# A decoder block on one core: fewer double seven-product units in FFN 1, one more in FFN 2, their products ordered by group, and three norms folded a step later

## The chip, the core and the metric

The kernel runs on one core of a Trainium2 chip. The metric is the device time of one execution in microseconds (us); lower is better. The core has a matrix engine (TensorE, PE in the profile, PEld for its weight loads), three elementwise engines (VectorE or DVE, ScalarE or ACT, GpSimd or POOL), and DMA queues, most of whose transfers are issued by SyncE (SP). Each engine works through its own instructions in their order and waits for the others by semaphores.

## The reference

One layer of a decoder block on 256 tokens of width 2048, in float32. What matters here are the two feed-forward parts at its ends, `h = h + 1/2 * SwiGLU(RMSNorm(h))`:

```python
def rms_norm(x, g):
    y = x * lax.rsqrt(jnp.mean(x * x, axis=-1, keepdims=True) + EPS)
    return y * g

def swiglu(x, w_gate, w_up, w_down):          # D_MODEL 2048, D_FF 5632
    return (jax.nn.silu(x @ w_gate) * (x @ w_up)) @ w_down
...
h = h + 0.5 * swiglu(rms_norm(h, ffn1_norm), ffn1_w_gate, ffn1_w_up, ffn1_w_down)
n = rms_norm(h, mix_norm)                     # retention and sliding-window attention, then w_out
h = h + memory_cross_attention(rms_norm(h, xa_norm), rms_norm(mem, mem_norm), ...)
h = h + 0.5 * swiglu(rms_norm(h, ffn2_norm), ffn2_w_gate, ffn2_w_up, ffn2_w_down)
```

## The kernel before

**Split operands.** Every operand of a matmul is split into a high half (a copy rounded to fp32r by ScalarE, L81) and a low half (what is left, by VectorE, L391). A product is three matmuls: high by high, high by low, low by high (`three`, L661 to 664). A weight arrives by DMA as a tile `wf` of 128x1024, and its split writes `wh` and `wl`.

**Steps.** All products stand in one long list of steps that `all_steps` (L336) makes. A plain step takes one weight tile, 2 token halves x 2 k-tiles x 3 = 12 matmuls of 128x512. `run_stream` (L404) walks the list. At each step it runs the tasks that are due, splits weights up to `LOOKAHEAD` = 3 steps ahead, issues loads up to 4 steps further ahead, then issues the step's matmuls. Tasks (`later`, L113) are pieces of work with a due time on a clock that counts 1 for a plain step and 0.5 for a chunk: copies, norms, transposes, sums. A scheduler then places the instructions on each engine.

**Units and twins.** The feed-forward parts work in units of 512 columns, 11 for gate and up and 4 for down. A `Twin` (L189) does gate and up of one unit (or two column blocks of down) together over four blocks of 512 rows of weights. A plain block costs 48 matmuls. One block, or two, is done in a seven-product way instead (Strassen's, in Winograd's form): it is seen as a 2 x 2 by 2 x 2 product (token halves, row halves, gate and up), which takes seven products, P1 to P7, each a chunk of 2 x 3 = 6 matmuls, 42 in all. For that VectorE forms differences of weights (L244, for P5, P6, P7 and P4), and seven tiles are split instead of four. P1, P3, P5 and P2 each load a tile; the others use differences. Sums of the inputs are made once per norm by `sums_of` (L309). After P1, P5, P6 and P7 of the last seven-product block, results are copied out of PSUM and added there (`keep`, `keep_other`, `middle`, `spread`, L272 to 286; adds on L265).

**Single and double units.** `sevens` (L740) is one block, or two when the unit's number is in `DOUBLE` (L39); the rest are plain. Chunks P1, P3, P5, P6, P7 of a unit are spread over the plain steps of the group ahead of it, P2 and P4 over its own (L363 to 372). `chunks` (L215) gives their order: kind by kind, and within a kind block by block. In FFN 1 `turned` is (2, 3), in FFN 2 (0, 1); units 4 and 8, which come right after a down part, are double in both.

**Norms.** `Norm.stat` sums squares on ScalarE and VectorE as blocks of `h` become ready. `Norm.finish` runs `delay` clock counts after the last of them: VectorE folds the sum (L593), TensorE adds over partitions with four tiny matmuls (L596), VectorE scales (L598), GpSimd takes the power -1/2 (L599). The matmuls of L596 stand in TensorE's order among the others, so TensorE waits there until the fold is done. The delays are 2 for `n1` (before FFN 1), 3 for `nmix` and 4 for `n2` (before FFN 2). The result is first used by the Silu of a gate (L710) or by a scaling copy.

Of the kernel before, what the change touches and what calls it, by code (L numbers as in the profile page):

```python
# [29 lines left out]
G_FFN1, G_MIX, G_XA, G_MEM, G_FFN2, G_GN = 0, 16, 32, 48, 64, 80  # L30
# [5 lines left out]
TURN = 6  # L36
SWA_EVERY = 4.5
LAND = 11
DOUBLE = (4, 8)  # L39
P1, P3, P5, P6, P7, P2, P4 = range(7)  # L40


# [1 line left out]
def decoder_block(ctx: ExitStack, tc: tile.TileContext, a: dict, out: bass.AP):  # L44
# [16 lines left out]
    def blk(dt=F32R):  # L61

        return work.tile([P, 4, 2, S], dt, tag="blk", name=nm("blk"), bufs=11)
# [4 lines left out]
    def t2k(dt=F32):  # L68
        return work.tile([P, 512], dt, tag="t2k", name=nm("t2k"), bufs=7)
# [10 lines left out]
    def copy(dst, src, **kw):  # L80
        return nc.scalar.activation(dst, src, AF.Copy, **kw)  # L81
# [31 lines left out]
    def later(delay, fn):  # L113
        tasks.append((clock[0] + delay, len(tasks), fn))
# [74 lines left out]
    class Twin:  # L189
# [23 lines left out]
            return self.plain[len(self.plain) - self.late :]  # L213

        def chunks(self, kinds):  # L215
            return [
                (self, c, None, kind, c == self.sevens[0], c == self.sevens[-1]) for kind in kinds for c in self.sevens
            ]

        def steps(self):  # L220
            return [
# [69 lines left out]
    def sums_into(s, v):  # L291

        for o, p, q, op in (
            (0, v(1, 0), v(1, 1), ALU.add), (1, s[:, 0], v(0, 0), ALU.subtract), (2, v(0, 0), v(1, 0), ALU.subtract),
            (3, v(0, 1), s[:, 1], ALU.subtract),
        ):
            dst = s[:, o]
            if len(q.shape) == 4:
                dst, p = (x.rearrange("p j (a b) -> p j a b", a=4) if len(x.shape) == 3 else x for x in (dst, p))
            elif len(p.shape) == 4:  # L300
                dst, q = (x.rearrange("p j (a b) -> p j a b", a=4) for x in (dst, q))
            nc.vector.tensor_tensor(dst, p, q, op)

    def split_sums(s):
        z = blk().rearrange("p k c s -> p (k c s)").rearrange("p (c i j s) -> p c i j s", c=2, i=4, j=2)
        halves(z[:, 0], z[:, 1], s)
        return z

    def sums_of(norm, b, dst, delay, src=None):  # L309

        y = [None]
        src = hT[b] if src is None else src

        def scale():
            y[0] = blk(F32).rearrange("p k c s -> p (k c s)")
            x = y[0][:, :1024].rearrange("p (j k s) -> p j k s", j=2, k=2)
            for k in range(4):
                g = norm.gcol + 4 * b + k
                copy(x[:, k % 2, k // 2, :], src[:, k, :], scale=gains[:, g : g + 1])

        def add():
            x = y[0][:, :1024].rearrange("p (j k s) -> p j k s", j=2, k=2)
            y.append(y[0][:, 1024:].rearrange("p (i j s) -> p i j s", i=4, j=2))
            sums_into(y[1], lambda t, k: x[:, :, k, t * P : (t + 1) * P])

        def part():
            dst[b] = split_sums(y[1])
        for i, fn in enumerate((scale, add, part)):
            later(delay + i, fn)

    def together(late=1):

        units[-2].then = units[-1]
        units[-2].late = units[-1].late = late
# [317 lines left out]
    def parts_of(x):  # L652
        return [x[:, :, c, :] for c in range(2)]

    def halves_of(out, x):
        for t in range(2):
            hi, lo = (y[:, :, t * P : (t + 1) * P].rearrange("p q (a j) -> p q a j", a=4) for y in x)
            halves(hi, lo, out[t])
        return x
# [35 lines left out]
    twins, input_sums = [], {}  # L695

    def twin(*args):

        twins.append(Twin(*args, ahead=bool(twins), spare=len(twins) % 2 == 0))

    def ffn(norm, w_gate, w_up, down, groups, turned):
        gated = {}
        made = {}
        acts = {}

        def gate_done(b, acc):
            assert norm.ready
            gated[b] = [t2k() for _ in range(2)]
            for t in range(2):
                nc.scalar.activation(gated[b][t], acc[t], AF.Silu, scale=norm.scale(t))  # L710

        def up_done(b, acc):
            s = gated.pop(b)
            for t in range(2):
                nc.vector.scalar_tensor_tensor(s[t], acc[t], norm.scale(t), s[t], ALU.mult, ALU.mult)
            turn(b, s)

        def both_done(b, f, acc):
            (gate_done, up_done)[f](b, acc)

        def turn(b, s):

            def made(out):
                acts[b] = blk()
                halves_of(out, parts_of(acts[b]))
                if b in starts:
                    y = blk(F32).rearrange("p k c s -> p (k c s)")[:, :1024].rearrange("p (i j s) -> p i j s", i=4, j=2)
                    sums_into(y, lambda t, k: out[t][:, 2 * k : 2 * k + 2])
                    asums[b] = split_sums(y)
            cross(s, made, TURN + (3 if b < 10 else 1))  # L730

        sums, asums = {}, {}
        twins.clear()
        input_sums[norm] = sums
        starts = [x[0] for x in groups]
        for g, fbs in enumerate(groups):
            for b in fbs:
                done = functools.partial(both_done, b)
                if b > 0:
                    sevens = turned[: 1 + (b in DOUBLE)]  # L740
                    plain = [x for x in range(4) if x not in sevens]
                    twin([w[2 * b : 2 * b + 2] for w in (w_gate, w_up)], norm.blocks, plain, sevens, sums, done)
                    if b == 1:
                        norm.bank = functools.partial(twins[0].bank, 0, 1)
                    continue
                for f, w in enumerate((w_gate, w_up)):
                    Unit(w, b, 512, norm.blocks, functools.partial(done, f), range(4), pair=True)
                if norm is not n1:
                    together(2)
            down(g, acts, fbs, asums)  # L750


    n1 = Norm(G_FFN1, "n1", 2)
    for b in range(4):
        if b > 0:
            later(4 * b - 1, lambda b=b: n1.block(b, [hT[b]]))
        later(4 * b + 2 * (b < 3), lambda b=b: n1.stat([hT[b]]))
    for at, b in ((8, 2), (40, 3)):
        later(at, lambda b=b: sums_of(n1, b, input_sums[n1], 0))

    def load_x(b, lo, hi):
        nc.sync.dma_start(hT[b][:, lo:hi, :], a["x"][b * P : (b + 1) * P, lo:hi, :])

    later(24, lambda: nc.sync.dma_start(sinks, a["sinks"]))

    nmix = Norm(G_MIX, "nmix", 3, spread=True)

    def near_mix(b):
        if b == 0:
# [6 lines left out]
    def ffn1_down(g, acts, fbs, sums):  # L776
        if g < 2:
            to_h(a["ffn1_w_down"], acts, 0.5, fbs, spare=3, seven=fbs[0], sums=sums)
        else:
            to_h(a["ffn1_w_down"], acts, 0.5, fbs, nmix, near_mix, seven=fbs[0], sums=sums)  # L780
            units[-2].rest = 4

    ffn(n1, a["ffn1_w_gate"], a["ffn1_w_up"], ffn1_down, (range(0, 4), range(4, 8), range(8, 11)), (2, 3))

# [400 lines left out]
    for i in range(4):  # L1187
        Unit(a["xa_wv"], i, 512, nmem.blocks, v_done(i), range(4))

    n2 = Norm(G_FFN2, "n2", 4)  # L1190
    to_h(a["xa_wo"], xo, 1.0, range(4), n2, lambda b: begin_ffn2(b), spare=2, seven=1, sums=osums, plain=2)
    units[-3].then, units[-3].lead = units[-2], 6

# [160 lines left out]
```

## Time and profile before

| | |
|---|---|
| Time, median of 3 runs | 2146.7 us (2138.54, 2146.7, 2147.3) |
| The profiled execution, its own time | 2140.22 us |
| its span | 2138.3 us |
| its mean granted TensorE clock | 0.997 |
| Instructions | 26847 |
| TensorE, busy | 2119.8 us, 99% of the span |
| VectorE, busy | 1698.5 us, 79% |
| ScalarE, busy | 1236.2 us, 58% |
| DMA | 482.61 MB, mean 226 GB/s |

In a row of the timeline the first two numbers are the start and the duration in us, then come engine, line and operation, tiles written and read without their numbers, shapes, and in brackets the idle time ahead of it on its engine and what ended it. In a row of waits: engine, tile and line that waited, what it waited for, the total, the number of times and the longest. The profile's line numbers are those of the kernel before.

### The profile page before, as it was taken

How to read it: one execution, taken by the hardware profiler on the slowest of the kernel's cores; microseconds unless marked ns; L12 is line 12 of the kernel's file. 1: busy time of each engine (PE TensorE's matmuls, PEld its weight loads, DVE VectorE, ACT ScalarE, POOL GpSimd, SP SyncE). 2: the span in 40 equal slices, each digit the busy share in tenths (PEclk: the TensorE clock that was granted, in tenths of full speed). 3: DMA queues.
4: the chain of work that ended last, by engine and by line, in shares of the span. 5: the costliest groups of instructions: out<-in, count | busy, mean ns of one | idle time of the engine just before them, and what ended most of it. 6: DMA issues, size and time to landing. Idle time of an engine off the chain costs nothing.

```text
span 2138.3 us, 26847 instructions
## 1 busy us (share of the span) xinstructions
PE 2119.8 (99%) x9564; PEld 1754.4 (82%) x9564; DVE 1698.5 (79%) x1997; ACT 1236.2 (58%) x1549; POOL 161.6 (8%) x273
## 2 busy tenths in 40 slices
PE   9999999999999999999999999999999999999998
PEld 7888788887888888878888888888888888888886
DVE  7887898778888788777887566578888888888875
ACT  6665565555666664546566454456666556555654
POOL 0000000000100210100101110011010000000000
PEclk9999999999999999999999999999999999999999
DMA  8677787777877876667878875586887677766773
GB/s 301 210 238 217 216 262 235 221 218 220 274 223 233 266 215 203 207 200 241 242 230 234 260 226 186 163 270 216 250 249 244 195 225 218 234 198 208 225 241 113
DMA packets 221286, 482.61 MB, mean 226 GB/s; under 512 B 18144, under 2 KB 18144, under 8 KB 221152
## 3 DMA queue, kind: packets, MB, share of 16 engines
q1 hardware_dynamic: 191312, 413.72, 61.6%
q0 software_dynamic: 12288, 33.57, 7.0%
q10 hardware_dynamic: 17552, 33.60, 4.3%
q8 instruction: 75, 1.23, 0.3%
q14 instruction: 59, 0.48, 0.1%
HBM read 445.17 MB, written 35.65 MB: 225 GB/s over the span
## 4 chain that ended last, share of the span: by engine, by line
PE 89%; DVE 5%; DMA 3%; issue 1%; ACT 1%; POOL 0%; DVEq 0%; ACTq 0%; POOLq 0%; SPq 0%
PE acc L664 55%; PE tmp L664 33%; DVE wl L391 2%; DMA wf<-in_ffn_w_up 1%; DMA wf<-in_ffn_w_gate 1%; DMA wf<-in_xa_wk 1%; ACT wh L81 1%; DVE blk L547 0%; DMA t4k<-box 0%; DMA wf<-in_ffn_w_down 0%; DVE t2k L585 0%; DVE h L679 0%; ACT blk L81 0%; DMA box<-t4k 0%; PE tmp L898 0%
## 5 line engine op out<-in xcount | busy, mean ns | idle before, releaser
L81 ACT ACTIVATE wh<-wf 128x1024 fp32r<-128x1024 f32 (+1 forms) x891 | 933.9, 1054 | 733.5 <-PE acc L664 416.6
L391 DVE TENSOR_TENSOR wl<-wf,wh 128x1024 fp32r<-128x1024 f32 (+1 forms) x886 | 1069.0, 1218 | 349.5 <-ACT wh L81 332.6
L664 PE MATMUL acc<-wh,blk 128*128 128x512 f32 (+1 forms) x3840 | 1211.8, 388 | 1.6 <-ACT wh L81 1.0
L664 PEld LDWEIGHTS acc<-wh,blk 128*128 128x128 f32 x3840 | 719.7, 188 | 151.4 <-ACT wh L81 2.0
L664 PE MATMUL acc<-wl,blk 128*128 128x512 f32 (+1 forms) x1920 | 744.5, 388 | 0.3 <-DVE wl L391 0.3
L664 PE MATMUL tmp<-wh,blk 128*128 128x512 f32 x2232 | 716.7, 390 | 0.0
L664 PEld LDWEIGHTS tmp<-wh,blk 128*128 128x128 f32 x2232 | 419.5, 188 | 87.5 <-ACT t2k L81 0.3
L664 PE MATMUL tmp<-wl,blk 128*128 128x512 f32 x1116 | 435.1, 390 | 2.5 <-DVE wl L391 2.5
L664 PEld LDWEIGHTS acc<-wl,blk 128*128 128x128 f32 x1920 | 361.8, 188 | 73.6 <-DVE wl L391 1.7
L647 POOL DMA_DIRECT2D t4k<-box x256 | 147.8, 584 | 1743.5 <-ACT wh L81 420.3
L664 PEld LDWEIGHTS tmp<-wl,blk 128*128 128x128 f32 x1116 | 209.8, 188 | 47.7 <-DVE wl L391 4.2
L244 DVE TENSOR_TENSOR wf<-wf,wf 128x1024 f32<-128x1024 f32 x152 | 185.9, 1223 | 31.3 <-DMA wf<-in_ffn_w_up 18.5
L81 ACT ACTIVATE t2k<-tmp 128x512 f32<-128x512 f32 x88 | 52.5, 597 | 33.6 <-PE tmp L664 21.1
L638 DVE STREAM_TRANSPOSE t4k<-t2k 128x512 f32<-128x512 f32 x96 | 64.5, 695 | 5.9 <-ACT t2k L81 5.5
L81 ACT ACTIVATE t2k<-acc 128x512 f32<-128x512 f32 x76 | 45.1, 596 | 29.7 <-PE acc L664 15.4
L86 DVE TENSOR_TENSOR blk<-t4k,blk 128x512 fp32r<-128x512 f32 (+2 forms) x72 | 44.3, 655 | 1.3 <-ACT blk L81 0.9
L81 ACT ACTIVATE blk<-t4k 128x512 fp32r<-128x512 f32 (+2 forms) x72 | 39.6, 595 | 3.3 <-DMA t4k<-box 2.6
L81 ACT ACTIVATE blk<-h,gains 128x256 fp32r<-128x256 f32 (+1 forms) x80 | 34.2, 496 | 11.6 <-DVE h L679 9.9
L265 DVE TENSOR_TENSOR tmp<-t2k,tmp 128x512 f32<-128x512 f32 x54 | 35.6, 690 | 0.0
L265 DVE TENSOR_TENSOR acc<-t2k,acc 128x512 f32<-128x512 f32 x48 | 31.7, 689 | 0.0
L547 DVE SCALAR_TENSOR_TENSOR blk<-h,gains,blk 128x256 fp32r<-128x256 f32 x64 | 26.8, 479 | 3.9 <-ACT blk L81 3.7
L679 DVE TENSOR_TENSOR h<-h,t4k 128x512 f32<-128x512 f32 x40 | 25.7, 684 | 2.7 <-DMA t4k<-box 2.7
(141 smaller groups left out, 607.7 us busy)
## 6 DMA issues: line engine op xcount, KB each, us to landing
wf<-in_ffn_w_gate SPq DMA_DIRECT2D x176, 512.0 KB, 5.1
wf<-in_ffn_w_up SPq DMA_DIRECT2D x176, 512.0 KB, 5.0
wf<-in_ffn_w_down SPq DMA_DIRECT2D x176, 512.0 KB, 4.6
box<-t4k ACTq DMA_DIRECT2D x64, 512.0 KB, 5.4
t4k<-box POOLq DMA_DIRECT2D x256, 128.0 KB, 7.1
wf<-in_w_in_rqk SPq DMA_DIRECT2D x32, 512.0 KB, 4.7
wf<-in_w_in_rvg SPq DMA_DIRECT2D x32, 512.0 KB, 4.7
wf<-in_w_out SPq DMA_DIRECT2D x32, 512.0 KB, 5.0
```

What stands on the lines that cost most here:

```text
L81: return nc.scalar.activation(dst, src, AF.Copy, **kw)
L86: nc.vector.tensor_tensor(lo, src, hi, ALU.subtract)
L244: nc.vector.tensor_tensor(dst, p, q, ALU.subtract)
L265: nc.vector.tensor_tensor(out, a, b, ALU.add)
L391: nc.vector.tensor_tensor(lo[:, cs], wf[:, cs], hi[:, cs], ALU.subtract)
L547: nc.vector.scalar_tensor_tensor(x[:, k, 1, :], v[:, k, :], g, x[:, k, 0, :], ALU.mult, ALU.subtract)
L638: nc.vector.transpose(z[:, t, :].rearrange("p (g q j) -> p q g j", g=4, q=4), squares_of(v))
L647: nc.gpsimd.dma_start(z[32 * g : 32 * g + 32].rearrange("p t (i n) -> p (t i) n", i=4), far[g])
L664: nc.tensor.matmul(o, x, y, start=first, stop=last, skip_group_check=shared)
L679: nc.vector.tensor_tensor(v, v, out[t], ALU.add)
```

## The change

Three things change. FFN 1 has one seven-product block in every unit (`turned` is (2,)), so its units 4 and 8 are no longer double, and the sums of its block 3 are no longer made. FFN 2 has a third double unit, 6. The chunks of a double unit come block by block (P1, P3, P5, P6 of the one, then of the other; P7 of both last), and so do P2 and P4. And the norms `n1`, `nmix` and `n2` have their `finish` one clock count later.

```diff
-DOUBLE = (4, 8)
+DOUBLE = (4, 6, 8)
...
         def chunks(self, kinds):
-            return [
-                (self, c, None, kind, c == self.sevens[0], c == self.sevens[-1]) for kind in kinds for c in self.sevens
-            ]
+            pairs = [(kind, c) for c in self.sevens for kind in kinds if kind != P7]
+            pairs += [(P7, c) for c in self.sevens if P7 in kinds]
+            return [(self, c, None, kind, c == self.sevens[0], c == self.sevens[-1]) for kind, c in pairs]
...
-                    sevens = turned[: 1 + (b in DOUBLE)]
+                    sevens = turned if b in DOUBLE else turned[:1]
...
-    n1 = Norm(G_FFN1, "n1", 2)
+    n1 = Norm(G_FFN1, "n1", 3)
...
-    for at, b in ((8, 2), (40, 3)):
-        later(at, lambda b=b: sums_of(n1, b, input_sums[n1], 0))
+    later(8, lambda: sums_of(n1, 2, input_sums[n1], 0))
...
-    nmix = Norm(G_MIX, "nmix", 3, spread=True)
+    nmix = Norm(G_MIX, "nmix", 4, spread=True)
...
-    ffn(n1, a["ffn1_w_gate"], a["ffn1_w_up"], ffn1_down, (range(0, 4), range(4, 8), range(8, 11)), (2, 3))
+    ffn(n1, a["ffn1_w_gate"], a["ffn1_w_up"], ffn1_down, (range(0, 4), range(4, 8), range(8, 11)), (2,))
...
-    n2 = Norm(G_FFN2, "n2", 4)
+    n2 = Norm(G_FFN2, "n2", 5)
```

Three places show how the instructions move. The first is TensorE at the statistic of `n1`, early in FFN 1. `acc` and `tmp` are PSUM tiles, `wh` and `wl` the halves of a weight, `blk` a block of the normed input. Before:

```order
L664 MATMUL acc_228<-wl_459,blk_423 128x512
L664 MATMUL acc_228<-wh_458,blk_423 128x512
L596 MATMUL tmp_469<-ones,t2k_216 128x1 x2
L664 MATMUL acc_228<-wh_458,blk_423 128x512
L664 MATMUL acc_228<-wl_459,blk_423 128x512
L664 MATMUL acc_228<-wh_458,blk_423 128x512
L664 MATMUL tmp_471<-wh_481,blk_402 128x512
```

Now the same stretch reads:

```order
L664 MATMUL acc_228<-wh_458,blk_423 128x512 x2
L664 MATMUL acc_228<-wl_459,blk_423 128x512
L664 MATMUL acc_228<-wh_458,blk_423 128x512
L664 MATMUL acc_160<-wh_497,blk_423 128x512
L664 MATMUL acc_160<-wl_498,blk_423 128x512
L664 MATMUL acc_160<-wh_497,blk_423 128x512 x2
L664 MATMUL acc_160<-wl_498,blk_423 128x512
L664 MATMUL acc_160<-wh_497,blk_423 128x512
L664 MATMUL acc_161<-wh_497,blk_423 128x512
L596 MATMUL tmp_469<-ones,t2k_216 128x1 x2
```

The statistic stands ten matmuls later, behind those with the low half `wl_498`, which came after it before.

The second is VectorE at the same place; L593 is the fold, L391 a low half, L244 a difference. Before:

```order
L244 TENSOR_TENSOR wf_432<-wf_432,wf_462 128x2x2x256
L391 TENSOR_TENSOR wl_498<-wf_464,wh_497 128x1024
L593 TENSOR_TENSOR t2k_216<-t2k_216 128x256
L391 TENSOR_TENSOR wl_517<-wf_432,wh_516 128x1024
L598 TENSOR_SCALAR ms_513<-tmp_469 128x2
```

Now:

```order
L244 TENSOR_TENSOR wf_432<-wf_432,wf_462 128x2x2x256
L391 TENSOR_TENSOR wl_498<-wf_464,wh_497 128x1024
L244 TENSOR_TENSOR wf_378<-wf_432,wf_378 128x2x2x256
L391 TENSOR_TENSOR wl_511<-wf_432,wh_510 128x1024
L593 TENSOR_TENSOR t2k_216<-t2k_216 128x256
```

A difference and a low half have moved ahead of the fold.

The third is VectorE in FFN 1's first down part, where the ahead chunks of unit 4 are made; `h` is the residual, to which a column block of down is added on L679. Before:

```order
L391 TENSOR_TENSOR wl_2060<-wf_1998,wh_2059 128x1024
L244 TENSOR_TENSOR wf_2131<-wf_2131,wf_1998 128x2x2x256
L391 TENSOR_TENSOR wl_2078<-wf_2016,wh_2077 128x1024
L391 TENSOR_TENSOR wl_2094<-wf_2033,wh_2093 128x1024
L244 TENSOR_TENSOR wf_2033<-wf_2033,wf_2097 128x2x2x256
L244 TENSOR_TENSOR wf_1950<-wf_2033,wf_1950 128x2x2x256
L391 TENSOR_TENSOR wl_2112<-wf_2051,wh_2111 128x1024
L679 TENSOR_TENSOR h_75<-h_75,t4k_1910 128x4x128 x2
```

Now the rows up to the same add:

```order
L391 TENSOR_TENSOR wl_2018<-wf_1938,wh_2017 128x1024
L391 TENSOR_TENSOR wl_2036<-wf_1969,wh_2035 128x1024
L391 TENSOR_TENSOR wl_2054<-wf_1986,wh_2053 128x1024
L391 TENSOR_TENSOR wl_2066<-wf_2004,wh_2065 128x1024
L391 TENSOR_TENSOR wl_2084<-wf_2021,wh_2083 128x1024
L679 TENSOR_TENSOR h_75<-h_75,t4k_1898 128x4x128 x2
```

The three differences ahead of the add are gone; the unit's one P5 difference stands eleven rows above the add, ahead of the low half `wl_1966`.

## The prediction

> **What bounds the kernel now.** I read the page first, then the table of waits of TensorE, then busy time by window, and last the timeline where TensorE waited. The page's first lines:
>
> ```profile
> span 2138.3 us, 26847 instructions
> PE 2119.8 (99%) x9564; PEld 1754.4 (82%) x9564; DVE 1698.5 (79%) x1997; ACT 1236.2 (58%) x1549; POOL 161.6 (8%) x273
> ```
>
> TensorE is busy in 99% of the span, so time can only come from fewer matmuls, from its 18.5 us of idleness, or from its clock. Its table of waits (total, times, longest):
>
> ```profile
> PE tmp L596 <- DVE t2k L593: 3.5, 3, 2.2
> PE tmp L664 <- DVE wl L391: 2.5, 4, 0.9
> ...
> PE acc L664 <- ACT t2k L81: 0.6, 1, 0.6
> ```
>
> The first row is the statistic of a norm, the second the low half of a weight, the third a copy out of PSUM. The windows show where the last two sit (length, then busy time of TensorE, its weight loads, VectorE, ScalarE and GpSimd with counts, granted clock, DMA share, GB/s):
>
> ```profile
> 100.00:150.00 50.00, 50.00 (x222) 41.42 (x221) 42.52 (x47) 31.85 (x39) 2.30 (x4) 1.00 0.76 228
> ...
> 1650.00:1700.00 50.00, 50.00 (x222) 41.40 (x221) 43.30 (x42) 28.44 (x29) 0.00 (x0) 1.00 0.60 190
> ...
> 1750.00:1800.00 50.00, 50.00 (x222) 41.42 (x221) 40.40 (x44) 29.55 (x33) 2.30 (x4) 1.00 0.79 227
> ...
> 250.00:255.00 5.00, 4.18 (x18) 3.30 (x18) 4.93 (x5) 2.37 (x3) 0.00 (x0) 1.00 0.48 140
> 255.00:260.00 5.00, 4.59 (x20) 3.62 (x20) 5.00 (x6) 2.29 (x3) 0.00 (x0) 1.00 0.35 107
> ...
> 275.00:280.00 5.00, 4.45 (x20) 3.36 (x20) 5.00 (x7) 3.32 (x5) 0.00 (x0) 1.00 0.73 229
> ...
> 500.00:505.00 5.00, 4.31 (x20) 3.22 (x18) 2.28 (x3) 3.00 (x4) 1.21 (x3) 1.00 1.04 261
> 505.00:510.00 5.00, 4.49 (x19) 3.37 (x19) 4.93 (x6) 2.36 (x3) 0.00 (x0) 1.00 0.37 111
> ```
>
> Undisturbed, TensorE issues 222 matmuls in 50 us, 0.2252 us each. In the five short windows the ahead products of FFN 1's double units 4 and 8 run, and TensorE idles for 0.82 + 0.41 + 0.55 + 0.69 + 0.51 = 2.98 us. Where those of FFN 2's unit 4 run (1650 to 1700) it does not idle.
>
> **Matmuls: +1.35 us.** A seven-product block issues 42 matmuls, a plain one 48. FFN 1 loses two such blocks, FFN 2 gains one: 6 more matmuls, 6 x 0.2252 = 1.35 us, all on the bound engine. There are 3 splits and 4 differences fewer.
>
> **FFN 1's double units: -2.98 us.** The timeline at unit 4:
>
> ```profile
> 248.40 1.23 DVE L244 TENSOR_TENSOR wf<-wf,wf 128x1024 f32<-128x1024 f32 x1 [2.08 <-DMA wf<-in_ffn_w_up]
> ...
> 250.82 0.50 PE L664 MATMUL tmp<-wl,blk 128*128 128x512 f32 x1 [0.87 <-DVE wl L391]
> ```
>
> The L244 is the second block's P5 difference. It held VectorE 2.08 us for a load, and the low half that TensorE wanted stood behind it. That instruction goes, and so do the differences that crowd VectorE at the adds to `h` after it (third place of the order). One P5 difference stays, earlier; it may wait for its own load, with a low half (`wl_1966`) behind it, but splits are made three steps ahead, 3 x 12 x 0.2252 = 8.1 us of TensorE's work. So I take all 2.98 us; the poor end is half of it.
>
> **The first norm: -3.1 us.** The timeline at its statistic, then the granted clock in quarters of a microsecond:
>
> ```profile
> 47.68 1.22 DVE L244 TENSOR_TENSOR wf<-wf,wf 128x1024 f32<-128x1024 f32 x1
> 47.87 0.40 PE L664 MATMUL acc<-wh,blk 128*128 128x512 f32 x1
> 48.81 1.22 DVE L391 TENSOR_TENSOR wl<-wf,wh 128x1024 fp32r<-128x1024 f32 x1
> ...
> 49.95 0.42 DVE L593 TENSOR_TENSOR t2k<-t2k 128x256 f32<-128x256 f32 x1
> ...
> 50.42 1.01 PE L596 MATMUL tmp<-ones,t2k 128*128 128x1 f32 x4 [2.16 <-DVE t2k L593]
> ...
> 51.29 0.77 PE L664 MATMUL acc<-wh,blk 128*128 128x512 f32 x1
> ...
> 51.71 1.62 POOL L599 TENSOR_TENSOR n<-ms,mhalf 128x2 f32<-128x2 f32 x1 [50.40 <-DVE ms L598]
> ...
> 57.34 0.62 PE L664 MATMUL acc<-wh,blk 128*128 128x512 f32 x2
> ...
> 57.84 0.69 ACT L710 ACTIVATE t2k<-acc,n 128x512 f32<-128x512 f32 x1 [0.78 <-PE acc L664]
> ```
>
> ```profile
> 50.25:50.50 0.25, 0.08 (x1) 0.08 (x1) 0.25 (x2) 0.00 (x0) 0.00 (x0) 0.83 0.40 156
> 50.50:50.75 0.25, 0.25 (x2) 0.25 (x2) 0.25 (x1) 0.00 (x0) 0.00 (x0) 0.50 0.74 287
> ...
> 57.00:57.25 0.25, 0.25 (x2) 0.25 (x1) 0.16 (x1) 0.06 (x1) 0.00 (x0) 0.51 0.97 303
> 57.25:57.50 0.25, 0.25 (x2) 0.21 (x2) 0.25 (x1) 0.00 (x0) 0.00 (x0) 1.00 1.04 311
> ```
>
> TensorE idles 2.16 us for the fold, which stands last in VectorE's backlog, and then the clock is halved from about 50.42 to 57.25, for 6.83 us. The two other statistics that TensorE waits for are those of `nmix` and `n2`:
>
> ```profile
> 744.99 0.61 PE L596 MATMUL tmp<-ones,t2k 128*128 128x1 f32 x4 [0.58 <-DVE t2k L593]
> ...
> 1467.01 0.58 PE L596 MATMUL tmp<-ones,t2k 128*128 128x1 f32 x4 [0.72 <-DVE t2k L593]
> 1467.45 0.48 PE L664 MATMUL tmp<-wh,blk 128*128 128x512 f32 x1
> ```
>
> The low clock costs: 14 matmuls between 51.29 and 57.34 took 6.05 us instead of 14 x 0.2252 = 3.15, and the statistic's own took 0.87 until the next matmul instead of 0.44 (at 1467.01): 2.90 + 0.43 = 3.3 us.
>
> The new order (first and second place) puts ten matmuls ahead of the statistic, 2.25 us, and a difference and a split ahead of the fold. It does not remove the wait. Of the ten, three run to about 48.77 and a fourth needs only a high half; the fifth needs the low half that VectorE ends at 48.81 + 1.22 = 50.03: a first wait of about 1.1 us. Six matmuls then end near 51.45. VectorE, busy throughout, begins an instruction every 1.14 us (48.81 to 49.95), so the fold begins at 49.95 + 2 x 1.14 = 52.23 and ends at 52.65: a second wait of about 1.25 us. Together 2.35 us, 0.19 more than before, but in two pieces with 1.35 us of matmuls between.
>
> What the clock makes of that no row shows. If it is judged by stretches of half the low time, 3.41 us, a stretch could before hold all 2.16 us of the gap; now the fullest holds 3.41 - 1.35 = 2.06, and when a border falls between the pieces, only some 1.2. So the bounds are 0.19 - 3.3 = -3.1 us (the clock holds) and +0.2 (it falls as before). I take -3.1, since most places of the border leave a stretch clearly less idle than the one that led to the half clock. The power on GpSimd ended at 51.71 + 1.62 = 53.33 and will end some 2.3 us later; its first reader, the gate's Silu, began at 57.84, so that hides.
>
> [...]
>
> **The other norms: -0.58 us.** For `nmix` the statistic stands 11 matmuls later (2.48 us) and the fold one split later (1.14 us): the wait of 0.58 us goes. For `n2` it is 20 matmuls (4.50 us) against 2 splits and 2 differences (4.56 us): the 0.72 us stay, 0. What else moves with a fold (the scaling, GpSimd's power, for `nmix` the spreading) moves by the same step.
>
> **FFN 2's third double unit and the order by groups: 0.** Unit 6's extra ahead products fall into 1750 to 1800: 5 splits and 3 differences, 8 x 1.14 = 9.1 us of VectorE beside 30 matmuls, 6.8 us. (40.40 + 9.1) / 56.8 = 87%, as in 1650 to 1700 (43.30 of 50), where nothing waits. That row is the nearest; the far end is unit 4 of FFN 1, 0.82 + 0.41 + 0.55 = 1.78 us. By groups, the six loads of a double unit are no longer in a row, and at most four differences follow each other instead of six: nothing waits in FFN 2's double units now, so there is nothing to gain; the far end is one wait like the 0.87 us above; 0 taken. The sums of FFN 1's fourth block, left out, ran beside a busy TensorE: 0.
>
> **Sum:** 1.35 - 2.98 - 3.1 - 0.58 + 0 = -5.3 us. The profiled execution took 2140.22 us, 6.5 below the median of the runs shown; I move the median: 2146.7 - 5.3 = **2141.4 us**.
>
> **Rivals.** *The clock still falls.* Either two waits of 2.35 us together are enough, or a wait of 2 us is not what halves the clock at all, and its cause stays. For it: 2.06 is hardly less than 2.16. Against: the border between stretches, and that the clock fell in the very quarter in which the wait ended. 2141.4 + 3.3 = 2144.7; chance 0.27. [...]
>
> *The waits only move.* VectorE loses 7 x 1.14 = 8 us of 1698.5; if its backlog is the cause, TensorE meets it elsewhere, and only the six matmuls count: 2146.7 + 1.35 = 2148.0; 0.13.
>
> *Slower: FFN 2's double units halve the clock.* If VectorE there falls back by 2.16 us in one place, that costs 2.16 + 3.3 = 5.5 us. One place takes the gain (+0.2); from the second on it decides: -5.3 + 11.0 = +5.7, 2152.4. For it: three double units and 87%. Against: no wait there now. 0.05.
>
> **How the numbers follow.** Forecast 0.5, the rivals 0.27, 0.13 and 0.05, 0.05 for the rest. The runs shown lie between 2138.54 and 2147.3, so a median can fall by that much by itself. Low end: the lowest run with the sum, and the waits left at `n1` and `n2` partly gone too: 2138.54 - 5.3 - 2.2 = 2131. High end: the second rival with 1.78 for the third double unit: 2150. A measurement can tell about 0.5%, 10.7 us, from no change. No case but the last rival doubled comes there by itself; the forecast does if the median falls at the lower end of the runs: faster 0.17, same 0.79, slower 0.04.
>
> **What would show it.** Right: no wait of TensorE near 250 and 505; two waits of about 1.1 and 1.25 us near 50, then clock 1.00; none near 745; no waits of TensorE between 1700 and 1825. Wrong: clock 0.50 after 52; waits on `wl` in FFN 2; a wait of 2 us or more at one place.

## The result, and the profile after

| | before | after |
|---|---|---|
| Median (lowest to highest) | 2143.38 us (2138.54 to 2147.3), 5 runs | 2160.5 us (2154.87 to 2165.0), 5 runs |
| The profiled execution, its span | 2140.22, 2138.3 us | 2154.87, 2153.1 us |

The change makes the kernel slower by a ratio of 1.0082 (95% interval 1.0055 to 1.0109), 17 us; 5 us faster was forecast. The profiled execution is the shortest of the five and 14.65 us above that of before. The first lines of the changed kernel's page, then its group of differences below that of the kernel before (count, busy time, mean ns of one, and the idle time of VectorE just ahead of them with what ended it):

```profile
span 2153.1 us, 26835 instructions
PE 2122.5 (99%) x9570; PEld 1754.5 (81%) x9570; DVE 1687.5 (78%) x1985; ACT 1229.7 (57%) x1541; POOL 159.6 (7%) x273
```

```profile
L244 DVE TENSOR_TENSOR wf<-wf,wf 128x1024 f32<-128x1024 f32 x152 | 185.9, 1223 | 31.3 <-DMA wf<-in_ffn_w_up 18.5 <-DMA wf<-in_xa_wk 6.6 <-DMA wf<-in_ffn_w_gate 2.2
L244 DVE TENSOR_TENSOR wf<-wf,wf 128x1024 f32<-128x1024 f32 x148 | 180.8, 1222 | 42.7 <-DMA wf<-in_ffn_w_up 31.8 <-DMA wf<-in_xa_wk 5.0 <-DMA wf<-in_ffn_w_gate 1.8
```

The counts are as costed: six matmuls more. VectorE has less to do than before and yet makes TensorE wait longer: it stands idle for 42.7 us ahead of its differences instead of 31.3, and 31.8 of them instead of 18.5 are for loads of the up weights. TensorE's table of waits:

```profile
PE tmp L664 <- DVE wl L391: 9.7, 3, 4.2
PE acc L664 <- DVE wl L391: 5.2, 5, 1.8
PE tmp L596 <- DVE t2k L593: 1.8, 2, 0.9
PE acc L664 <- ACT t2k L81: 1.6, 3, 1.1
```

The low halves went up from 2.5 us, the statistics of the norms went down from 3.5. To see where, I cut both spans at the same events, the product of up and gate (L715) of a unit. The windows from FFN 1's unit 3 to 4, 4 to 8, and FFN 2's unit 4 to 7; first before:

```profile
189.49:318.29 128.80, 126.97 (x558) 104.13 (x557) 110.01 (x111) 76.05 (x85) 11.51 (x20) 1.00 0.78 237
318.29:572.05 253.76, 252.56 (x1112) 208.10 (x1111) 211.90 (x215) 149.78 (x167) 18.43 (x32) 1.00 0.77 233
...
1735.94:1861.50 125.56, 125.56 (x555) 103.97 (x554) 101.95 (x106) 73.66 (x82) 6.91 (x12) 1.00 0.75 225
```

and after:

```profile
186.53:321.51 134.98, 129.44 (x559) 106.30 (x558) 102.50 (x104) 72.54 (x81) 11.50 (x20) 0.97 0.75 226
321.51:582.26 260.75, 255.13 (x1117) 210.49 (x1116) 204.54 (x209) 146.68 (x163) 18.41 (x32) 0.99 0.75 226
...
1748.21:1875.69 127.48, 124.79 (x549) 102.67 (x548) 109.52 (x113) 76.51 (x85) 6.91 (x12) 1.00 0.72 222
```

Up to unit 3 the changed kernel is 189.49 - 186.53 = 2.96 us ahead. Then the first down part with unit 4 takes 6.18 us more, the stretch to unit 8 with the second down part 6.99, FFN 2's third double unit 1.92; what lies between adds the rest. In the first of these TensorE idles 134.98 - 129.44 = 5.54 us (1.83 before), in the second 5.62 (1.20 before). Here is the first down part, on SyncE, VectorE and TensorE:

```profile
228.80 0.37 SPq L381 DMA_DIRECT2D wf<-in_ffn_w_up  x1
...
229.75 0.71 DVE L638 STREAM_TRANSPOSE t4k<-t2k 128x512 f32<-128x512 f32 x1 [0.36 <-ACT t2k L81]
...
233.91 0.84 PE L664 MATMUL tmp<-wh,blk 128*128 128x512 f32 x3
...
236.59 1.23 DVE L244 TENSOR_TENSOR wf<-wf,wf 128x1024 f32<-128x1024 f32 x1 [6.12 <-DMA wf<-in_ffn_w_up]
...
237.73 1.22 DVE L391 TENSOR_TENSOR wl<-wf,wh 128x1024 fp32r<-128x1024 f32 x1
...
239.00 0.80 PE L664 MATMUL tmp<-wl,blk 128*128 128x512 f32 x1 [4.25 <-DVE wl L391]
```

The difference at 236.59 is unit 4's P5. Its load was issued at 228.80. VectorE arrived at 230.47, 1.7 us later, and stood 6.12 us. The low half behind it needed nothing from that load (its high half, by the order of the splits, was ready at 230.67); it came at 238.95, and TensorE waited 4.25 us for it. The clock then:

```profile
235.00:237.50 2.50, 0.00 (x0) 0.00 (x0) 0.91 (x1) 1.34 (x2) 0.60 (x2) 0.95 0.59 225
237.50:240.00 2.50, 1.00 (x2) 0.83 (x3) 2.50 (x4) 0.00 (x0) 2.50 (x5) 0.50 0.65 167
240.00:242.50 2.50, 2.50 (x7) 1.98 (x6) 2.50 (x4) 0.00 (x0) 1.50 (x3) 0.50 0.89 257
242.50:245.00 2.50, 2.50 (x9) 1.96 (x8) 1.05 (x1) 0.90 (x1) 0.00 (x0) 0.69 1.07 235
```

It is at 0.50 from 237.23 to 244.06, while TensorE waits and for some 5 us more. The same pair stands in the second down part: VectorE waits 5.72 us for unit 8's P5 at 497.64, TensorE 3.85 us at 500.06. Units 5 and 9 add waits of 1.29 and 1.77 us at 285.12 and 545.86.

Before, the two P5 differences of unit 4 ran as follows (the second was shown with the prediction):

```profile
234.91 0.37 SPq L381 DMA_DIRECT2D wf<-in_ffn_w_up  x1
...
239.64 0.37 SPq L381 DMA_DIRECT2D wf<-in_ffn_w_up  x1
```

```profile
241.69 1.23 DVE L244 TENSOR_TENSOR wf<-wf,wf 128x1024 f32<-128x1024 f32 x1 [2.08 <-DMA wf<-in_ffn_w_up]
```

VectorE came to them at 239.61 and 246.32, 4.7 and 6.7 us after their loads had been issued, and waited 2.08 us for each. In all three cases the data came 6.8 to 8.8 us after the issue; the changed kernel's page has a median of 4.9 us for the loads of the up weights.

The norms, on TensorE of the changed kernel: the statistic of `n1`, and those of `nmix` and `n2`:

```profile
50.22 0.50 PE L664 MATMUL acc<-wl,blk 128*128 128x512 f32 x1 [0.99 <-DVE wl L391]
...
52.82 0.61 PE L596 MATMUL tmp<-ones,t2k 128*128 128x1 f32 x4 [0.93 <-DVE t2k L593]
...
758.62 0.59 PE L596 MATMUL tmp<-ones,t2k 128*128 128x1 f32 x4
...
1481.75 0.50 PE L664 MATMUL acc<-wl,blk 128*128 128x512 f32 x1 [0.96 <-DVE wl L391]
...
1483.31 0.58 PE L596 MATMUL tmp<-ones,t2k 128*128 128x1 f32 x4 [0.83 <-DVE t2k L593]
```

At `n1` two waits of about 1 us stand in place of 2.16, and the clock stays at 1.00. At `nmix` nothing waits. At `n2` a wait on a low half has joined the one on the fold. FFN 2's third double unit has two waits that no double unit had before:

```profile
1771.24 0.50 PE L664 MATMUL tmp<-wl,blk 128*128 128x512 f32 x1 [1.57 <-DVE wl L391]
...
1795.77 0.50 PE L664 MATMUL acc<-wh,blk 128*128 128x512 f32 x1 [1.11 <-ACT t2k L81]
```

### The profile page after: what moved, and what is told of

Its sections match the earlier page's. It is cut to its first block, busy times and chain, and to the rows that moved or that the text cites. A ratio compares the mean times of both kernels' runs of the same rounds, so it can differ in the third digit from the quotient of the medians.

```text
span 2153.1 us, 26835 instructions
## 1 busy us (share of the span) xinstructions
PE 2122.5 (99%) x9570; PEld 1754.5 (81%) x9570; DVE 1687.5 (78%) x1985; ACT 1229.7 (57%) x1541; POOL 159.6 (7%) x273
## 4 chain that ended last, share of the span: by engine, by line
PE 89%; DVE 4%; DMA 4%; issue 2%; ACT 1%; POOL 0%; SPq 0%; DVEq 0%; ACTq 0%; POOLq 0%
PE acc L664 55%; PE tmp L664 33%; DVE wl L391 2%; DMA wf<-in_ffn_w_up 2%; DMA wf<-in_ffn_w_gate 1%; ACT wh L81 1%; DMA t4k<-box 0%; DVE wf L244 0%; DMA box<-t4k 0%; DMA h<-in_x 0%; PE tmp L897 0%; DVE blk L547 0%; PE tmp L878 0%; DVE h L679 0%; PE tmp L971 0%
## 5 line engine op out<-in xcount | busy, mean ns | idle before, releaser
L391 DVE TENSOR_TENSOR wl<-wf,wh 128x1024 fp32r<-128x1024 f32 (+1 forms) x883 | 1064.9, 1218 | 357.3 <-ACT wh L81 344.9
L244 DVE TENSOR_TENSOR wf<-wf,wf 128x1024 f32<-128x1024 f32 x148 | 180.8, 1222 | 42.7 <-DMA wf<-in_ffn_w_up 31.8
L679 DVE TENSOR_TENSOR h<-h,t4k 128x512 f32<-128x512 f32 x40 | 25.7, 683 | 3.5 <-DMA t4k<-box 3.5
```

What stands on the lines that cost most here:

```text
L244: nc.vector.tensor_tensor(dst, p, q, ALU.subtract)
L391: nc.vector.tensor_tensor(lo[:, cs], wf[:, cs], hi[:, cs], ALU.subtract)
L679: nc.vector.tensor_tensor(v, v, out[t], ALU.add)
```

## The experiments

The theory after these traces: the scheduler puts a difference far ahead of the split that needs it; where the difference reads a tile that its own chunk has just loaded, VectorE stands still for the load, and everything behind it is late. I call that hoisting. The rivals: the order by groups, the third double unit or the delayed norms make the loss; or each wait is local and can be mended by itself.

**FFN 1's single units alone**, on the kernel before:

```diff
-    for at, b in ((8, 2), (40, 3)):
-        later(at, lambda b=b: sums_of(n1, b, input_sums[n1], 0))
+    later(8, lambda: sums_of(n1, 2, input_sums[n1], 0))
...
-                    sevens = turned[: 1 + (b in DOUBLE)]
+                    sevens = turned if b in DOUBLE else turned[:1]
...
-    ffn(n1, ..., (range(0, 4), range(4, 8), range(8, 11)), (2, 3))
+    ffn(n1, ..., (range(0, 4), range(4, 8), range(8, 11)), (2,))
```

> The kernel before with one part of the change alone: FFN 1 with single units only. Theory (in FFN 1 the P5 difference of units 4 and 8 now stands far ahead in VectorE's order, waits about 6 us there for its load, TensorE waits about 4 us behind it, and the clock halves): this part alone costs 2 x 7 = 14 us against before, waits of TensorE of 3.5 to 4.5 us near 235 and 495, VectorE idle 5 to 6 us on a load ahead of each. Rival (the loss is made in FFN 2 by the third double unit, or by the folds): -1.6 us or no change, and no wait of TensorE over 1 us in FFN 1 but at the first norm.

Measured: 2159.85 us against 2140.76 for the kernel before on the same chip, ratio 1.0087 (1.0075 to 1.0099). TensorE's waits:

```profile
PE tmp L664 <- DVE wl L391: 7.1, 2, 3.6
PE acc L664 <- DVE wl L391: 5.3, 2, 2.7
```

They stand at 237.63 (3.61), 284.00 (2.59), 500.19 (3.47) and 546.78 (2.68 us), each behind a P5 difference that VectorE waited for (5.49, 4.46, 5.34 and 4.55 us): those of units 4, 5, 8 and 9. This part alone makes a loss as large as the whole change's: 0.0087 x 2140.76 = 19 us, of which the twelve matmuls more (9576) are an estimated 12 x 0.2252 = 2.7. The theory's 14 us did not count units 5 and 9.

**The changed kernel with FFN 1's double units back:**

```diff
-                    sevens = turned if b in DOUBLE else turned[:1]
+                    sevens = turned if b in (DOUBLE if norm is not n1 else (4, 8)) else turned[:1]
```

with the sums of block 3 and (2, 3) as before.

> The changed kernel with FFN 1's units 4 and 8 double again, all else as changed (order by groups, third double unit in FFN 2, folds one step later). Theory: the two long waits in FFN 1 go, 14 us less than the changed kernel, so within 5 us of before. Rival (FFN 2 or the folds): stays about 17 us above before.

Measured: 2146.49 us, ratio 1.0018 (1.0006 to 1.003). Most of the 17 us is gone. 0.0018 x 2140.76 = 3.9 us are left, and the largest row of waits is a new one, on ScalarE's copies out of PSUM:

```profile
PE acc L664 <- ACT t2k L81: 6.0, 5, 1.8
```

**Two differences held.** In the changed kernel the P5 differences of FFN 1's units 4 and 8 may not go ahead of the VectorE instruction written just before them:

```diff
+            last, n = look(), seen[0]
             nc.vector.tensor_tensor(dst, p, q, ALU.subtract)
+            if kind == P5 and self.hold:
+                for ins in nc.cur_bb.bb.instructions[n:]:
+                    if ins.engine in anchored and ins.engine in last:
+                        order(last[ins.engine], ins)
...
+                    twins[-1].hold = norm is n1 and b in (4, 8)
```

`look` gives the last instruction of each engine so far, `order` keeps two in their order.

> The changed kernel with one more rule: the P5 differences of FFN 1's units 4 and 8 may not be placed ahead of the VectorE instruction that the program issues before them, which moves each about 11 rows later, behind ten low halves. Nothing else changes. Theory (the place of the difference is the cause): VectorE waits less than 1 us for each load, the waits of TensorE of 4.25 and 3.85 us and the low clocks behind them go, 10 to 14 us less than the changed kernel. Rival (the load itself is late, wherever the difference stands): the wait moves to the place of the P5 product or its split, TensorE still waits 2 us or more near 240 and 500, and the time stays within 4 us of the changed kernel.

Measured: 2151.68 us, ratio 1.005 (1.0037 to 1.0064). No wait is left near 237 and 500, but unit 5's P5 difference now waits longer, first on VectorE, then on TensorE:

```profile
277.13 1.23 DVE L245 TENSOR_TENSOR wf<-wf,wf 128x1024 f32<-128x1024 f32 x1 [5.09 <-DMA wf<-in_ffn_w_up]
```

```profile
279.55 0.79 PE L669 MATMUL acc<-wl,blk 128*128 128x512 f32 x1 [3.22 <-DVE wl L396]
```

Unit 9 does the same (2.56 us at 538.12). FFN 2's third double unit, which the edit leaves alone, shows a wait of 3.11 us on a copy at 1791.68 (1.11 in the changed kernel), after a difference that VectorE waited 3.26 us for. About half came back, and in FFN 1 the waits moved to the next hoisted differences. That each wait can be mended by itself is out.

**All differences held**, in the changed kernel: the same edit without its condition.

> The changed kernel with that rule for every difference: each now stands 1 to 6 rows ahead of its own split instead of 3 to 21. Theory: besides the two waits of FFN 1, VectorE's other waits for loads (5.0 us at the first unit of FFN 2, 4.0 us at the third double unit) shrink, and with them most of the waits of TensorE in FFN 2: at or below before, 14 to 20 us less than the changed kernel. Rival (a difference so near to its split stands in the way of it): new waits of TensorE at the products P5 to P7, time between before and the changed kernel or above.

Measured: 2132.3 us, ratio 0.996 (0.9948 to 0.9972): below both kernels, and (1.0082 - 0.996) x 2140.76 = 26 us below the change as it was. The group of differences (L244 is L245 here) and the two windows that hold the 4 us waits in the changed kernel:

```profile
L245 DVE TENSOR_TENSOR wf<-wf,wf 128x1024 f32<-128x1024 f32 x148 | 180.2, 1218 | 0.0
```

```profile
200.00:250.00 50.00, 50.00 (x222) 41.44 (x221) 39.62 (x40) 29.12 (x34) 4.62 (x8) 1.00 0.81 242
450.00:500.00 50.00, 50.00 (x222) 41.43 (x221) 38.88 (x39) 29.03 (x34) 6.93 (x12) 1.00 0.78 250
```

VectorE waits for no load ahead of a difference any more (42.7 us before the edit), and TensorE does its full 222 matmuls in 50 us. In VectorE's order, unit 4's P5 stood eleven rows ahead of the add to `h`; held, it stands two rows behind it, and begins at 247.77, 17.1 us after its load was issued (230.68).

**The three norms alone**, on the kernel before (the three delays, nothing else):

```diff
-    n1 = Norm(G_FFN1, "n1", 2)
+    n1 = Norm(G_FFN1, "n1", 3)
...
-    nmix = Norm(G_MIX, "nmix", 3, spread=True)
+    nmix = Norm(G_MIX, "nmix", 4, spread=True)
...
-    n2 = Norm(G_FFN2, "n2", 4)
+    n2 = Norm(G_FFN2, "n2", 5)
```

> The kernel before with the three norms' folds one step later and nothing else. Theory (the delays do what the prediction says of them): two waits of about 1 us near 50 us and no half clock after them, no wait at the statistic of nmix near 745, the one at n2 as before; -0.24 - 3.3 - 0.58 = -4.1 us against the kernel before, a ratio of about 0.998. Rival (the loss of the whole change has a share here, since each fold shifts differences and splits behind it): a wait of 2 us or more somewhere in the three stages and a ratio of 1.000 to 1.002.

Measured: 2138.86 us against 2140.49, ratio 0.9986 (0.9976 to 0.9996), so 0.9 to 5.1 us. Near 50 the waits are 0.92 and 0.95 us with the clock at 1.00, none is left at `nmix`, and the one at `n2` is 0.83. The theory stands. The profile also has waits outside the three norms, the longest 1.98 us at 1039.37 in the cross-attention with 3.41 us of half clock behind it: VectorE had stood 8.27 us there at a difference for a load of `in_xa_wk`. In the kernel before the same place has 6.59 us on VectorE and 0.31 on TensorE.

**The third double unit alone**, on the kernel before, in its order by kind:

```diff
-                    sevens = turned[: 1 + (b in DOUBLE)]
+                    sevens = turned[: 1 + (b in DOUBLE + (6,) * (norm is not n1))]
```

> The kernel before with FFN 2's unit 6 made double, in the old order by kind, and nothing else. Theory (the waits of 1.57 and 1.11 us that the changed kernel shows at its third double unit come from the order by groups and from a difference put far ahead): six matmuls fewer, no wait over 0.5 us between 1700 and 1830, -1.35 us, a ratio of 0.999. Rival (the double unit itself is too much for VectorE there): waits of 1.5 to 3 us there and +0.5 to +2 us, a ratio of 1.000 to 1.001.

Measured: 2142.35 us, ratio 1.0001 (0.9989 to 1.0013). Between 1700 and 1830 there is one wait, of 0.35 us at 1772.84. So the unit by itself makes no waits of the kind seen in the changed kernel; its 1.35 us are below what the runs can tell. Far from unit 6, the profile has a wait of 3.54 us at the statistic of `nmix` (746.53), which is no difference's: the fold was late because an add to `h` ahead of it had waited 3.22 us for a DMA (`t4k<-box`), where the kernel before waited 0.25.

**The order by groups alone**, on the kernel before:

```diff
-            return [
-                (self, c, None, kind, c == self.sevens[0], c == self.sevens[-1]) for kind in kinds for c in self.sevens
-            ]
+            pairs = [(kind, c) for c in self.sevens for kind in kinds if kind != P7]
+            pairs += [(P7, c) for c in self.sevens if P7 in kinds]
+            return [(self, c, None, kind, c == self.sevens[0], c == self.sevens[-1]) for kind, c in pairs]
```

> The kernel before with the products of double units in the order by groups and nothing else. Theory (the order by groups asks for the copies out of PSUM sooner, and TensorE waits for ScalarE's copy t2k): waits of 1.4 to 1.9 us on t2k in double units, as where the changed kernel had its double units back, 5 of them in all; +3 to +6 us, a ratio of 1.0015 to 1.003. Rival (the order by groups costs nothing; those waits came from the other parts): the waits of the kernel before and a ratio within 0.001 of 1.

Measured: 2145.53 us, ratio 1.0022 (1.0011 to 1.0034). Three waits on a copy, 5.2 us in all: 2.67 us at 278.37 and 1.82 at 533.11, in FFN 1's double units, and 0.70 at 1700.30 in FFN 2. What made the first copy late, on ScalarE and on VectorE:

```profile
277.72 0.60 ACT L81 ACTIVATE t2k<-acc 128x512 f32<-128x512 f32 x1 [3.79 <-DVE acc L265]
```

```profile
272.39 1.23 DVE L244 TENSOR_TENSOR wf<-wf,wf 128x1024 f32<-128x1024 f32 x1 [2.72 <-DMA wf<-in_ffn_w_gate]
...
277.00 0.69 DVE L265 TENSOR_TENSOR acc<-t2k,acc 128x512 f32<-128x512 f32 x1
```

The copy waited for an add on VectorE, and VectorE had stood 2.72 us at a difference for its load, a few instructions earlier. The row of waits names ScalarE; the source is a difference once more, and the copy at 533.11 has the same chain, with 1.88 us. The load is of the gate weights, so this is no P5 but a P4 (the last of the unit's eight differences), which reads the tile that the P2 just ahead of it loads.

**All differences held in the kernel before**, with the edit of the changed kernel:

> The kernel before with no difference put ahead of the VectorE instruction that was written just before it. Theory (what makes TensorE wait in both kernels is the hoisting of differences ahead of work whose data is there): the waits of 0.4 to 0.9 us in FFN 1's double units shrink, and most of what the changed kernel so held gained comes without the change: -4 to -8 us, 2133 to 2137 us. Rival (the gain of the changed kernel so held is the change's own, whose loss the holding only uncovered): before so held stays within 2 us of the kernel before.

Measured: 2130.65 us, ratio 0.9951 (0.9939 to 0.9964). Against the changed kernel so held (0.996) the intervals overlap: with hoisting gone the change is worth nothing that can be measured, and hoisting costs an estimated (1 - 0.9951) x 2140.49 = 10 us in the kernel before and 26 in the changed one.

**The kernel before once more**, unedited, for a second profile:

> The kernel before once more, unedited, for a second profile of it. Theory (the halving of the clock is a matter of chance for waits between about 1.5 and 2.7 us, long enough only where a stretch of the throttle happens to fall on them): a wait of 1.7 to 2.2 us at the statistic of n1 near 50 us as in the first profile, but as likely with the clock at 1.00 behind it as at 0.50. Rival (the wait decides): 0.50 again for 6.8 us whenever the wait is over 1.9 us, 1.00 whenever it is under that. The time itself: a ratio of 1.000, which shows what five rounds resolve.

Measured: 2141.38 us, ratio 1.0002 (0.999 to 1.0014). The statistic of `n1`, then the clock around it:

```profile
49.81 0.61 PE L596 MATMUL tmp<-ones,t2k 128*128 128x1 f32 x4 [1.80 <-DVE t2k L593]
```

```profile
48.00:50.00 2.00, 0.20 (x3) 0.20 (x2) 2.00 (x4) 1.06 (x1) 0.00 (x0) 1.00 0.33 109
50.00:52.00 2.00, 2.00 (x12) 1.70 (x12) 2.00 (x3) 0.70 (x1) 0.96 (x1) 1.00 0.84 225
52.00:54.00 2.00, 2.00 (x10) 1.67 (x9) 1.69 (x3) 1.73 (x3) 0.66 (x1) 1.00 0.68 247
```

The same instructions wait 1.80 us here and the clock stays. By itself this fits the rival too. But with the old fold the kernels of the single units and of the order by groups waited 1.93 and 1.79 us there at a full clock, and elsewhere in the latter 2.67 us left it at 1.00, while 1.53 us halved it in the kernel before with its differences held. The length of the wait alone does not decide; the last section has what does.

**Only P5 held**, in the changed kernel (`if kind == P5:` around the edit's loop):

> The changed kernel with all P5 differences, and only those, not ahead of the VectorE instruction written just before them; P6, P7 and P4 are placed as in the changed kernel. Theory (a hoisted difference costs when it reads a tile loaded for its own chunk, which among the ahead chunks P5 alone does): no wait of VectorE over 2 us on a load left, the waits near 237, 284, 500 and 546 us gone, most of the 28 us between the changed kernel and its version with all held come back: 2133 to 2140 us, a ratio to before of 0.996 to 1.000. Rival (what costs is the crowding of VectorE by any hoisted difference): waits of 2 us or more stay or move again, as when only two were held, and the time stays above 2145 us.

Measured: 2133.2 us, ratio 0.9966 (0.9954 to 0.9978). P6, P7 and P4 may be hoisted as before, and nearly everything is back. (None can stand ahead of its P5, since P6 reads what P5 writes, and P7 and P4 what P6 writes. But they do come sooner: unit 4's P4 stands 10 rows behind its P5 here, 24 where all are held.)

```profile
L245 DVE TENSOR_TENSOR wf<-wf,wf 128x1024 f32<-128x1024 f32 x148 | 180.3, 1218 | 1.6 <-DMA wf<-in_ffn_w_gate 0.4
```

So it is not the crowding of VectorE by differences. It is the one kind among the ahead chunks that reads a tile loaded for its own chunk. (P4, late in the order by groups alone, is not held here; all waits for gate tiles in this row are 0.4 us.)

**The change without its single units, all differences held**, first in the order by kind (the kernel before with the edit to all differences, the three delays and the third double unit):

> The kernel before with all differences held, the three norms a step later and FFN 2's third double unit, in the old order by kind. Theory (with the hoisting gone the terms add up: six matmuls fewer than the kernel before so held, and the wait of 1.53 us at nmix with the half clock that it sometimes brings gone): 2126 to 2130 us, 1 to 4 us below the kernel before so held. Rival (what is left is not in VectorE's order, and the third double unit makes waits): 2130 to 2134 us.

Measured: 2132.0 us, ratio 0.9967 (0.9955 to 0.998); the theory's 2126 to 2130 is missed. The time lies in the rival's range, but its reason does not show: the longest wait of TensorE at the third double unit is 0.74 us. Then in the order by groups:

> As the run before it, but with the products of the double units in the order by groups. Theory (by groups TensorE asks for ScalarE's copies t2k sooner than they are made): waits of 0.5 to 1.8 us on t2k in the five double units, +2 to +5 us against the order by kind, 2129 to 2134 us. Rival (those waits came with the hoisted differences too): within 1 us of the order by kind.

Measured: 2129.95 us, ratio 0.9957 (0.9944 to 0.9971). The waits on copies are gone, as the rival has it, and the theory's 2 to 5 us against the order by kind did not come: the median is 2.05 us lower, more than the rival's 1 us, but the ratios' intervals overlap. The order by groups costs nothing that can be measured once the differences are held. The four kernels with all differences held lie within 2.4 us of each other, with overlapping intervals. Which of them is best stays open. Seven to ten us below the kernel before is what holding gives (0.9967 to 0.9951), and the rest of the change moves it by less than can be told.

## Why the prediction was wrong

- *Matmuls, +1.35 us.* Right: 9570 against 9564.
- *FFN 1's double units, -2.98 us: the step that failed.* In the prediction's words: "One P5 difference stays, earlier; it may wait for its own load, with a low half (`wl_1966`) behind it, but splits are made three steps ahead, 3 x 12 x 0.2252 = 8.1 us of TensorE's work. So I take all 2.98 us". The place, the instruction and the half behind it were the right ones. The 8.1 us of cover were not there. VectorE came to the difference at 230.47. Without a wait it would have been through with it in 1.14 us and with the low half 1.22 us later, at 232.83; TensorE wanted it at 239.00 - 4.25 = 234.75. So the cover was 1.9 us. The wait was 6.12, and 6.12 - 1.9 = 4.2 is what TensorE waited. I took the lead from the program's distance between split and use, where the trace of before has the moments; and I gave the wait no size at all, where the row at 248.40 had one: an instruction that reaches its load 2 us too soon. In its new place VectorE came to it 1.7 us after the issue of its load instead of 4.7 and 6.7. Units 5 and 9, whose differences also moved, were not looked at. With the clock, this term was +13 us by the windows (6.18 + 6.99) and +19 by the run of this part alone (0.0087 x 2140.76) instead of -2.98; both hold matmuls that the prediction had priced apart, 2.7 us in the run.
- *The first norm, -3.1 us.* Right in its waits (1.1 and 1.25 forecast, 0.99 and 0.93 found) and in the clock of both profiles that have it, of the changed kernel and of the norms alone. Wrong in what it is worth: the 3.3 us of half clock were those of one execution. In four other profiles with the old fold (waits 1.93, 1.80, 1.79 and 1.06 us) the clock did not fall there, so in the first profile it had fallen by the place of a border: the stretch from 47.00 to 50.42 held all 2.16 us there (last section). The delays together measured 0.9 to 5.1 us, so a gain is there; its share by the clock is not separated.
- *`nmix`, -0.58 us.* Right in the changed kernel and with the norms alone. In another execution with the same delay (all held, order by groups) 1.73 us are back, where the add to `h` had waited 2.78 us for a DMA; the delay does not cover that. *`n2`, 0.* A second wait of 0.96 us came ahead of the fold's; missed, small.
- *The third double unit and the order by groups, 0.* The first was right by itself (1.0001). The second measured 1.0022, 4.7 us, but 4.5 of its 5.2 us of waits stand in FFN 1's double units, which the changed kernel does not have. In FFN 2 the two together were wrong: the changed kernel's third double unit waits 1.57 and 1.11 us, 2.7 in all, as much as the two far ends together (1.78 and 0.87) where 0 was taken, and the second of these waits is on a copy, which no bound named.
- *The sum* was put on a median of 2146.7 of three runs; 29 runs on another chip give 2140.49. That is 6 us which no part of the change explains.
- *The rivals.* The slower one (2152.4, 0.05) had the mechanism: VectorE falls back in one place, TensorE waits, the clock halves, and from the second place on it decides. It looked for it in FFN 2's double units, the fuller ones. It was in FFN 1's single units, whose P5 differences stand further ahead. That VectorE, with less to do there, also ran ahead to the load was not tested apart.

The parts measured alone add up to 2140.5 x (0.0087 - 0.0014 + 0.0001 + 0.0022) = 20.5 us; together they measured 17.6. That these are near is no proof that they add: most of the last part's waits have no place in the changed kernel. What makes the scheduler place P5 so far ahead is not settled here: the runs take its freedom away, they don't show what it weighs.

## What to carry to other kernels

VectorE ran its instructions in their order, and an instruction moved ahead of work whose data is there was a bet on its load: unit 4's P5 stood 6.12 us, and the low half behind it, which needed nothing from that load, came 4.25 us late for TensorE. Read the bet from the trace: the moment when the engine gets there, the moment when the load was issued and how long such loads take, and the moment when the other engine wants what stands behind. A lead counted in the program's steps is no substitute. And look at the order anew when work is taken away: here VectorE had less to do, and what was left was placed so that it met its loads sooner (1.7 us after the issue instead of 4.7 and 6.7).

A row of waits names the last link. Here the long ones under "<- ACT t2k" and "<- DVE wl" were a difference that stood for a DMA, which only that difference's own idle time showed (31.8 us for the up weights). Under "<- DVE t2k", some were an add to `h` that stood for another DMA.

## What the runs showed of the hardware

- In the 14 profiles of this case the granted clock was halved 16 times between the first 20 us and the last matmul, each time for 3.41 or 6.83 us. All seven waits of 3.1 us or more halved it, no wait under 1.5 us did, and of 19 between 1.5 and 2.7 us 9 did. Which of these did went by borders in these profiles. Within a profile the drops begin whole multiples of 3.413 us apart: in the changed kernel those at 237.23 and 500.06 lie 262.83 us apart, 77 lengths of the short one, so 3.413 us each; with the order by groups alone, the one at 533.38 and the one after the last matmul, at 2137.64, are 470.0 such stretches apart. On that grid, two waits of this profile:

```profile
273.97:277.38 3.41, 1.73 (x8) 1.11 (x6) 3.41 (x5) 0.00 (x0) 0.00 (x0) 1.00 0.38 129
277.38:280.79 3.41, 2.42 (x11) 2.01 (x12) 3.16 (x4) 2.22 (x3) 0.00 (x0) 1.00 0.59 192
...
529.97:533.38 3.41, 1.58 (x7) 1.03 (x6) 3.41 (x5) 0.93 (x2) 0.00 (x0) 1.00 0.57 174
533.38:536.79 3.41, 3.41 (x9) 2.64 (x9) 1.91 (x3) 1.50 (x2) 0.00 (x0) 0.50 0.87 244
```

The wait of 2.67 us was cut by a border into 1.68 and 0.99, and the clock stayed; the shorter one, of 1.82, lay whole in one stretch, and the next stretch ran at half clock. Laid so over all 14 profiles, each of the 16 drops follows a stretch at full clock in which, for 1.82 us or more, no matmul ran but those of a statistic (one column wide), and no stretch at full clock with 1.77 us or less was followed by one. This sorting was found afterwards, and it needs the statistics counted as idleness: by the waits alone, a stretch with 1.50 us led to half clock and one with 1.76 did not. Where the grid falls differs from profile to profile: borders stand at 47.00 and 50.42 in the kernel before, at 49.50 and 52.91 in the changed one. So a wait of 2 us cost 2 us here or, by an estimate of 3.3 / 2 = 1.7 us for one stretch at half clock (3.3 us for the two near 50 in the first profile), some 4.
- Two waits of about 1 us (0.99 and 0.93 with 1.67 us between them in the changed kernel, 0.92 and 0.95 with 1.66 in the norms alone) left the clock at 1.00 in each of the profiles that had them at `n1`. The prediction's stretches of 3.41 us were an estimate, half of the one low of 6.83 us. The reasoning with them held, but its size did not: its fullest stretch, 2.06 us, would have been over that border. In the changed kernel the matmuls between the waits took 1.67 us instead of 1.35, and the fullest stretch (49.50 to 52.91) came to 1.74, just under it. That is luck.
- The spread between executions was a result too. The kernel before ran from 2135.17 to 2147.57 us (23 runs), two of the held kernels from 2131.58 to 2132.52 and from 2131.59 to 2132.44 (5 runs each). In the two held kernels whose `nmix` still waits, the profiled execution took 2134.04 and 2133.93 us against 2129.47 to 2130.86 otherwise, and its profile has one wait there (1.53 and 1.73 us) and one stretch at half clock. The other executions have no profile, so that this is the difference is likely but not shown. In both profiles the fold stood behind an add to `h` that had waited for a DMA, 1.21 and 2.78 us.

```profile
736.91 0.63 PE L600 MATMUL tmp<-ones,t2k 128*128 128x1 f32 x4 [1.53 <-DVE t2k L597]
```

```profile
735.00:737.00 2.00, 0.47 (x3) 0.09 (x1) 1.86 (x3) 1.06 (x1) 0.00 (x0) 1.00 0.19 56
737.00:739.00 2.00, 2.00 (x8) 1.71 (x9) 1.30 (x2) 0.00 (x0) 1.17 (x1) 0.59 0.81 227
739.00:741.00 2.00, 2.00 (x7) 1.57 (x6) 0.00 (x0) 0.00 (x0) 0.47 (x1) 0.56 0.93 274
```

These are rows of the kernel before with its differences held.
